# Four token tiles in flight in place of three in the first stage of a streaming encoder layer

## The chip, the core and the metric

The kernel runs on one core of a Trainium2 chip. The metric is the device time of one execution in microseconds (us). The five engines of the core are called TensorE (PE), VectorE (DVE), ScalarE (ACT), GpSimd (POOL) and SyncE (SP, which here issues all transfers). Each has its own queue and works through it in order.

## What is computed

One inference step of one layer over 1,024 prompt tokens and 32 sample tokens, 1,024 channels wide. Cut to what matters here:

```
h   = RMSNorm(x)                        # times the gains g_mix_norm
z   = h @ w_in                          # 1024 x 8192: q, k, v of both branches, gates
o_a = DiffAttn(h)                       # 8 heads, chunk-causal, two softmax maps per head
o_r = Retention(h)                      # 8 heads, rotary, chunkwise recurrent
x   = x + (sigmoid(g_a) * o_a + sigmoid(g_r) * o_r) @ w_o
x   = x + SwiGLU(RMSNorm(x))
x   = x + sigmoid(RMSNorm(x) @ w_ple_gate) * (p @ w_ple)
```

The outputs are the new x of all tokens, the new keys and values, and the retention states.

## The kernel before, in words

**Numbers.** Inputs are float32. For TensorE every operand is split into two float16 parts, a high one (a cast, mostly on ScalarE) and a low one (the rest, on VectorE), and a product takes three matmuls: high by high, high by low, low by high (lines 723, 724, 725). Each 256-column block of weights first needs a scale, from the sum of its squares (ScalarE, line 416, then a small matmul, line 300, and a chain of tiny VectorE instructions); then four parts of 512 columns per block are cast (ScalarE, line 462) and their low parts taken (VectorE, line 464).

**The stages.** The tokens stand in nine tiles of 128 rows (the last, of 32 rows, is the sample). For each of 8 heads, the program projects the tiles by the head's A half of w_in (q, k, v of the attention, q, k of the retention) and its B half (v of the retention and three gates), and does the attention and the retention of each tile. Then follow the products by w_o, the feed-forward part and the last gate. The change concerns the beginning: the stretch of some 85 us in which head 0 can work only on tiles that have been prepared.

**Preparing a token tile (`norm_x`, line 649).** The tile x*i* is loaded (line 662), squared and summed (ScalarE, 668), multiplied by the gains `gb` (GpSimd, 673; tile x0 alone on VectorE, 682), its inverse root taken (GpSimd, 758 and 759), scaled (ScalarE 687 or VectorE 689), transposed in two halves of four 128-column transposes each (TensorE, 697), and each half is cast (line 388) and its low part taken from PSUM (VectorE, 708). Slots for tiles lie in one weight buffer, `xw`: three for tiles and a fourth for `gb`. A tile waits for the tile three before it to be done, and, from x4 on, for the projection of tile *i*-4 (`("wait", ("pA", i - 3))`).

**What sets the order of the work.** The steps of all these parts are Python generators. A planner (`Flow`, line 86) runs them against its own clock: each step names an engine and an estimated cost, `("get", ...)` takes a buffer, `("wait", ...)` an event, `("delay", ...)` stands for a transfer's time, and of the steps that are ready the one that can start first is emitted, ties going to the lower priority number. So costs, delays and priorities decide only the order in which each engine's queue is written; the chip runs each queue in that order. Steps of a weight block take priority 2 as long as its due number lies more than 4 (`FAR`) ahead of the projection now under way, and -2 from then on (in `load_block_steps`). Projections of head 0 go A0, A1, A2, A3, A4, B0, A5, B1 and so on (`LAG` = 4): one of them is 8 steps of three matmuls.

Step counts below count these steps of three matmuls from the first projection on: A0 to A3 are steps 1 to 32, A4 is 33 to 40, and the 41st is B0's first. "Half" is one half of a token tile, four transposes.

## Time and profile before

| what | us |
|---|---|
| three timed runs, median (lowest to highest) | 1947.84 (1945.46 to 1948.18) |
| the profiled execution | 1947.6 |
| its span, first to last instruction | 1945.8 |
| TensorE busy in the span | 1885.6 (97%) |
| VectorE busy | 1531.5 (79%) |
| ScalarE busy | 1065.3 (55%) |
| GpSimd busy | 697.0 (36%) |

The span is what the trace covers; 1.8 us of the execution lie around it. The page of the profile divides the span into 40 slices of 48.6 us: TensorE is busy 5 tenths of the first, 8 of the second and 9 or more of all others but two in the middle, which belong to the passage into the feed-forward part. A view of stretches gives the same by any window, a view in order of time gives single instructions, and a view of waits says what ended an engine's idle time.

### The profile page before, as it was taken

To read this page: it belongs to the slowest core of one execution; us is meant where nothing else is said; L and a number is where in the kernel's file an instruction comes from. 1 tells how busy PE (TensorE), PEld (TensorE's weight loads), DVE (VectorE), ACT (ScalarE), POOL (GpSimd) and SP (SyncE) were. 2 spreads that over 40 slices of the span, in tenths; PEclk is the share of its full clock that TensorE was granted. 3 is DMA by queue.
4 is the path that set the end of the run, shared out by engine and by line. 5 is a ranking of instruction groups with operands and counts; after the bars stand their busy time and mean duration, and the time that the engine had idled before them with its cause. 6 is when DMAs were issued, how large, how long until landed. Compare 5 with 4: busy or idle time off the path is not lost.

```text
span 1945.8 us, 38415 instructions
## 1 busy us (share of the span) xinstructions
PE 1885.6 (97%) x14267; PEld 1216.2 (63%) x14267; DVE 1531.5 (79%) x3995; ACT 1065.3 (55%) x2775; POOL 697.0 (36%) x1142
## 2 busy tenths in 40 slices
PE   5899999999999999999999998899999999999999
PEld 2465565555655555556556685777777776666665
DVE  7887878788878788878888579999999986753364
ACT  6676767666666666666665346555555552111132
POOL 3754444344454444444543048323223210000010
PEclk9899999999999999999999999999999999999999
DMA  5221202112121121120213721122211107211031
GB/s 194 72 72 53 83 20 72 56 49 63 33 76 59 28 79 41 52 81 18 75 57 127 268 71 34 72 94 81 74 66 45 66 31 261 78 60 61 28 131 49
DMA packets 71949, 147.44 MB, mean 76 GB/s; under 512 B 25265, under 2 KB 52017, under 8 KB 63825
## 3 DMA queue, kind: packets, MB, share of 16 engines
q1 hardware_dynamic: 71760, 144.98, 22.3%
q8 instruction: 112, 1.84, 0.4%
q14 instruction: 77, 0.62, 0.1%
HBM read 113.61 MB, written 31.34 MB: 74 GB/s over the span
## 4 chain that ended last, share of the span: by engine, by line
PE 83%; DVE 10%; ACT 2%; POOL 2%; issue 2%; DMA 1%; SPq 0%; DVEq 0%; POOLq 0%; ACTq 0%
PE pj L723 10%; PE pj L725 9%; PE pj L724 9%; PE ps L471 9%; PE ps L473 9%; PE ps L472 9%; PE ps L1458 4%; PE ps L1456 4%; PE ps L1457 4%; PE t L907 2%; PE sc L860 2%; PE sc L863 1%; PE pj L734 1%; PE t L1055 1%; PE po L926 1%
## 5 line engine op out<-in xcount | busy, mean ns | idle before, releaser
L723 PE MATMUL pj<-w,xh 128*128 128x512 f16 x1024 | 390.6, 381 | 0.7 <-ACT w L462 0.7
L724 PE MATMUL pj<-w,xh 128*128 128x512 f16 x1024 | 389.8, 381 | 1.4 <-DVE w L464 1.4
L725 PE MATMUL pj<-w,xh 128*128 128x512 f16 x1024 | 389.8, 381 | 0.0
L471 PE MATMUL ps<-mixs,w 128*128 128x352 f16 (+1 forms) x960 | 260.6, 277 | 1.5 <-DVE pws L1336 1.5
L472 PE MATMUL ps<-mixs,w 128*128 128x352 f16 (+1 forms) x960 | 260.5, 276 | 0.3 <-POOL mixs L1482 0.3
L473 PE MATMUL ps<-mixs,w 128*128 128x352 f16 (+1 forms) x960 | 260.4, 276 | 0.0
L471 PEld LDWEIGHTS <-w 128*128 128x128 f16 x1728 | 169.7, 98 | 65.6 <-issue 7.0
L473 PEld LDWEIGHTS <-w 128*128 128x128 f16 x1728 | 169.4, 98 | 55.1 <-issue 4.2
L472 PEld LDWEIGHTS <-w 128*128 128x128 f16 x1728 | 169.5, 98 | 49.6 <-issue 0.8
L725 PEld LDWEIGHTS <-xh 128*128 128x128 f16 x1024 | 100.5, 98 | 124.3 <-DVE xh L708 2.5
L1591 POOL TENSOR_TENSOR st<-st 128x512 f32<-128x512 f32 x66 | 85.9, 1301 | 251.5 <-DVE w L1586 187.0
L723 PEld LDWEIGHTS <-xh 128*128 128x128 f16 x1024 | 101.3, 99 | 77.5 <-issue 1.1
L878 ACT ACTIVATE p<-sc,nb,scs 128x256 f32<-128x256 f32 (+7 forms) x128 | 106.1, 830 | 77.6 <-DVE nb L872 29.9
L472 PE MATMUL ps<-tT,w 128*128 128x352 f16 (+1 forms) x528 | 143.6, 277 | 3.6 <-DVE tT L1482 3.6
L724 PEld LDWEIGHTS <-xh 128*128 128x128 f16 x1024 | 100.5, 98 | 72.7 <-issue 0.8
L473 PE MATMUL ps<-tT,w 128*128 128x352 f16 (+1 forms) x528 | 143.7, 277 | 0.0
L471 PE MATMUL ps<-tT,w 128*128 128x352 f16 (+1 forms) x528 | 143.6, 277 | 0.0
L1586 DVE SCALAR_TENSOR_TENSOR w<-st,gus,w 128x512 f16<-128x512 f32 x132 | 140.4, 1064 | 0.1
L870 DVE TENSOR_REDUCE nm<-sc 128x1 f32<-128x768 f32 (+6 forms) x112 | 102.5, 916 | 27.0 <-PE sc L863 25.5
L1458 PE MATMUL ps<-a,w 128*128 128x352 f16 x312 | 97.5, 313 | 0.5 <-DVE w L1677 0.5
L1457 PE MATMUL ps<-a,w 128*128 128x352 f16 x312 | 97.5, 313 | 0.0
L1456 PE MATMUL ps<-a,w 128*128 128x352 f16 x312 | 97.5, 312 | 0.0
(433 smaller groups left out, 4890.0 us busy)
## 6 DMA issues: line engine op xcount, KB each, us to landing
st<-in_win_dram SPq DMA_DIRECT2D x30, 1024.0 KB, 4.9
st<-in_wgu_dram SPq DMA_DIRECT2D x22, 1024.0 KB, 4.9
st<-in_wdn_dram SPq DMA_DIRECT2D x16, 704.0 KB, 4.5
out_dram<-kv SPq DMA_DIRECT2D x64, 128.0 KB, 1.7
a_d<-a SPq DMA_DIRECT2D x9, 528.0 KB, 2.6
b<-a_d SPq DMA_DIRECT2D x9, 528.0 KB, 8.5
mixs<-mix_d SPq DMA_DIRECT2D x8, 528.0 KB, 6.2
pw_d<-pws SPq DMA_DIRECT2D x12, 352.0 KB, 5.6
```

What stands on the lines that cost most here:

```text
L471: nc.tensor.matmul(out=ps, lhsT=wh, rhs=ah, start=first, stop=False)
L472: nc.tensor.matmul(out=ps, lhsT=wh, rhs=al, start=False, stop=False)
L473: nc.tensor.matmul(out=ps, lhsT=wl, rhs=ah, start=False, stop=last)
L723: nc.tensor.matmul(out=ps, lhsT=xhi, rhs=w[:, k, 0], start=(k == 0), stop=False)
L724: nc.tensor.matmul(out=ps, lhsT=xhi, rhs=w[:, k, 1], start=False, stop=False)
L725: nc.tensor.matmul(out=ps, lhsT=xh[:, k, 1, t0:t0 + P], rhs=w[:, k, 0], start=False, stop=(k == KD - 1))
L870: nc.vector.tensor_reduce(out=nm[0:R, mc], in_=pv, axis=AX.X, op=ALU.max, negate=True)
L878: nc.scalar.activation(pt[0:R, 0:NK], ps[0:R, p0:p0 + NK], AF.Exp, bias=nb[0:R, m:m + 1], scale=sc_ap[0:R], accum_out=Z[0:R, m:m + 1])
L1456: nc.tensor.matmul(out=ps, lhsT=wt[:, 0, j], rhs=a[:, 0, cs], start=(first and j == js[0]), stop=False)
L1457: nc.tensor.matmul(out=ps, lhsT=wt[:, 1, j], rhs=a[:, 0, cs], start=False, stop=False)
L1458: nc.tensor.matmul(out=ps, lhsT=wt[:, 2, j], rhs=a[:, 1, cs], start=False, stop=(last and j == js[-1]))
L1586: nc.vector.scalar_tensor_tensor(out=w[:, i, 1], in0=src, scalar=s, in1=w[:, i, 0], op0=ALU.mult, op1=ALU.subtract)
```

## The change

In `norm_x`, four slots hold token tiles, so a tile waits for the one four before it, and the wait for the projection is gone; the gains lie in the buffer that later holds the cached keys of the sample (`kcs`), so the first writing of that buffer now waits for the last token tile. The load of the first B weights waits until tile x3 has landed, and their due number is 9 where it was 4, so that their steps keep priority 2 during steps 1 to 40. The planner takes 3.0 in place of 2.0 for the time of a weight block's or a token tile's transfer. The loads of some small constants (`const_b`) are no longer held until x0 has been scaled, but until it is done.

```
--- before.py
+++ after.py
@@ -402,7 +402,7 @@
         else:
             yield DM(1.0)
             nc.sync.dma_start(out=st, in_=src)
-            yield ("delay", 2.0)
+            yield ("delay", 3.0)
         norm = rowf is None and not tail
         am4 = sm(4, "wam4", 3)
         am8 = sm(8, "wam8%d" % b, 1) if rowf is not None else None
@@ -526,7 +526,7 @@
         nc.gpsimd.memset(s02[64:128], 0.0)
 
         xw = wtile().bitcast(F32)
-        gb = xw[:, 3 * D:4 * D]
+        gb = hp.tile([P, 4, PAST], F16, tag="kcs", name="gb").rearrange("p m c -> p (m c)").bitcast(F32)
         xdone = []
         gsc = ca.tile([P, 3], F32, name="gsc")
 
@@ -568,7 +568,7 @@
 
         def const_b():
 
-            yield ("wait", ("n", 0))
+            yield ("wait", ("x", 0))
             yield ("get", "th")
             yield ("get", "z")
             rows_sb = wk.tile([P, 3, P], F32, tag="th", name="th").rearrange("p a c -> p (a c)")
@@ -649,18 +649,17 @@
         def norm_x(i):
 
             R = P if i < NT - 1 else TS
-            if i > 2:
-                yield ("wait", ("x", i - 3))
             if i > 3:
-                yield ("wait", ("pA", i - 3))
+                yield ("wait", ("x", i - 4))
             if i == 2:
                 yield DM(0.3)
                 nc.sync.dma_start(out=cs_sb, in_=rot)
             yield ("get", "xc")
-            xf = xw[:, i % 3 * D:(i % 3 + 1) * D]
+            xf = xw[:, i % 4 * D:(i % 4 + 1) * D]
             yield DM(R / 256.0)
             nc.sync.dma_start(out=xf[0:R], in_=xN[i, 0:R])
-            yield ("delay", 2.0)
+            yield ("delay", 3.0)
+            yield ("set", ("xd", i))
             yield ("get", "p")
             yield S(D, 0.1)
             sq = pp_.tile([P, 1024], F32, tag="p", name="xsq")
@@ -826,8 +825,7 @@
             nc.vector.tensor_scalar(out=do_s, in0=p2[:, 1:2], scalar1=lun, scalar2=_f(2.0 ** -14), op0=ALU.mult, op1=ALU.mult)
             vsc = sm(1, "vsc")
             nc.vector.tensor_tensor(out=vsc, in0=dA[1], in1=s[:, 1:2], op=ALU.mult)
-            if h:
-                yield ("wait", ("av", h - 1, NT - 1))
+            yield ("wait", ("av", h - 1, NT - 1) if h else ("x", NT - 1))
             kcs = hp.tile([P, 4, PAST], F16, tag="kcs", name="kcs")
             vcs = hp.tile([P, 4, 2, P], F16, tag="vcs", name="vcs")
             for m in range(2):
@@ -1232,6 +1230,8 @@
         def load_w(h, ab, res, prio, split=False):
 
             def steps(b0, b1):
+                if ab and not h:
+                    yield ("wait", ("xd", 3))
                 if b0 == 0:
                     yield ("get", "w")
                     res.extend(pair_tile())
@@ -1239,7 +1239,7 @@
                 yield ("wait", ("wt", ab, h))
                 for b in range(b0, b1):
                     yield from load_block_steps(win[h, 2 * ab + b], res[0], b, 0, "wAB"[1 + ab], None, res[1],
-                                                due=h * NT + ab * LAG)
+                                                due=h * NT + ab * (LAG if h else 9))
                     yield ("set", ("w", ab, h, b))
             if split:
                 flow.add(steps(0, 1), prio)
@@ -1417,7 +1417,7 @@
                 flow.add(ple(part), 6)
 
         flow = Flow(dict(pj=3, sc=1, o=3, p=5, A=5, B=3, w=3, st=2, mix=4, z=3, kv=3, rot=2, sqz=2, qst=2, q4=2, aT=2, of=2,
-                         ret=2, th=2, xc=3, su=1))
+                         ret=2, th=2, xc=4, su=1))
         flow.buffers["w"].pop()
         with tc.manual_schedule(engines={mybir.EngineType.PE, mybir.EngineType.DVE, mybir.EngineType.Activation,
                                          mybir.EngineType.Pool}):
```

The engines' queues change as follows at the three places that the prediction speaks of. TensorE's queue, where it passes from the fourth projection to the fifth (rows of line 697, 696 after the change, are transposes of token tiles, the others projections); first before, from the end of step 31 on:

```order
L725 LDWEIGHTS xh
L725 MATMUL pj<-w,xh 128x512
L723 LDWEIGHTS xh
L723 MATMUL pj<-w,xh 128x512
L724 LDWEIGHTS xh
L724 MATMUL pj<-w,xh 128x512
L725 LDWEIGHTS xh
L725 MATMUL pj<-w,xh 128x512
L697 MATMUL t<-cst_sb,w 128x128 x16
L723 LDWEIGHTS xh
L723 MATMUL pj<-w,xh 128x512
L724 LDWEIGHTS xh
```

and with the change, from the end of step 34 on:

```order
L724 LDWEIGHTS xh
L724 MATMUL pj<-w,xh 128x512
L696 MATMUL t<-cst_sb,w 128x128 x4
L722 LDWEIGHTS xh
L722 MATMUL pj<-w,xh 128x512
L723 LDWEIGHTS xh
L723 MATMUL pj<-w,xh 128x512
L724 LDWEIGHTS xh
L724 MATMUL pj<-w,xh 128x512
L696 MATMUL t<-cst_sb,w 128x128 x8
L722 LDWEIGHTS xh
L722 MATMUL pj<-w,xh 128x512
```

Before, a block of sixteen transposes (four halves, x4's first) stands in one piece behind step 32. With the change, halves of x4 and x5 stand singly behind steps 21, 29, 31 and 34, and a block of eight (two halves) behind step 35.

GpSimd's queue behind its first pair of roots (lines 673 and 672 are the multiplications of a token tile by the gains, 758, 759 and 757, 758 the roots of tiles, 959 to 967 the rotary of head 0); before:

```order
L673 TENSOR_TENSOR w<-w 128x1024
L758 TENSOR_SCALAR xss<-xss 128x1
L759 TENSOR_TENSOR xnr<-xss,neghalf 128x1
L673 TENSOR_TENSOR w<-w 128x1024
L758 TENSOR_SCALAR xss<-xss 128x1
L759 TENSOR_TENSOR xnr<-xss,neghalf 128x1
L673 TENSOR_TENSOR w<-w 128x1024
L758 TENSOR_SCALAR xss<-xss 128x1
L759 TENSOR_TENSOR xnr<-xss,neghalf 128x1
L959 TENSOR_TENSOR ta<-zr,cs_sb 128x128
L963 TENSOR_TENSOR tb<-zr,cs_sb 128x128
L965 TENSOR_TENSOR qk<-ta,tb 128x2x32
```

and with the change:

```order
L672 TENSOR_TENSOR w<-w,gb 128x1024 x2
L757 TENSOR_SCALAR xss<-xss 128x1
L758 TENSOR_TENSOR xnr<-xss,neghalf 128x1
L672 TENSOR_TENSOR w<-w,gb 128x1024
L757 TENSOR_SCALAR xss<-xss 128x1
L758 TENSOR_TENSOR xnr<-xss,neghalf 128x1
L757 TENSOR_SCALAR xss<-xss 128x1
L758 TENSOR_TENSOR xnr<-xss,neghalf 128x1
L672 TENSOR_TENSOR w<-w,gb 128x1024
L757 TENSOR_SCALAR xss<-xss 128x1
L758 TENSOR_TENSOR xnr<-xss,neghalf 128x1
L672 TENSOR_TENSOR w<-w,gb 128x1024
```

The multiplications of x1 and x2 now stand together, those of x3, x4 and x5 follow, all ahead of any rotary; before, a tile's rotary stood behind the fourth root.

VectorE's queue in the middle of the A weights' low parts (line 464, `A0s` and `A1s` for the two blocks; 708 and 707 are low parts of token halves, 689 and 688 a tile's scaling); before:

```order
L708 TENSOR_TENSOR xh<-t,xh 128x4x128
L583 TENSOR_SCALAR gS<-gS 128x8
L464 SCALAR_TENSOR_TENSOR w<-st,A0s,w 128x2x256
L464 SCALAR_TENSOR_TENSOR w<-st,A1s,w 128x2x256
L585 TENSOR_SCALAR gd<-gd 128x1
L678 TENSOR_SCALAR xrg<-xnr,gsc 128x1
L589 TENSOR_REDUCE gam<-th 128x2
L464 SCALAR_TENSOR_TENSOR w<-st,A0s,w 128x2x256
L464 SCALAR_TENSOR_TENSOR w<-st,A1s,w 128x2x256
L708 TENSOR_TENSOR xh<-t,xh 128x4x128
L464 SCALAR_TENSOR_TENSOR w<-st,A0s,w 128x2x256
L464 SCALAR_TENSOR_TENSOR w<-st,A1s,w 128x2x256
```

and with the change:

```order
L464 SCALAR_TENSOR_TENSOR w<-st,A1s,w 128x2x256
L388 CAST xh<-t 128x4x128
L464 SCALAR_TENSOR_TENSOR w<-st,A0s,w 128x2x256
L464 SCALAR_TENSOR_TENSOR w<-st,A1s,w 128x2x256
L707 TENSOR_TENSOR xh<-t,xh 128x4x128
L560 CAST id_88<-cst_sb 128x128
L464 SCALAR_TENSOR_TENSOR w<-st,A0s,w 128x2x256
L464 SCALAR_TENSOR_TENSOR w<-st,A1s,w 128x2x256
L677 TENSOR_SCALAR xrg<-xnr,gsc 128x1
L688 TENSOR_SCALAR w<-w,xrg 128x1024
L464 SCALAR_TENSOR_TENSOR w<-st,A1s,w 128x2x256
```

The scaling of x1 has come into VectorE's queue ahead of the last low part, and a first instruction on a constant (line 583) has gone behind them.

## Rows read from the trace of the kernel before

**Rows 1.** First line of the page.
```profile
span 1945.8 us, 38415 instructions
```

**Rows 2.** Stretches: from:to, length, busy us of each engine, clock of TensorE, transfers.
```profile
core 0: us, PE busy (x) PEld busy (x) DVE busy (x) ACT busy (x) POOL busy (x), PEclk, DMA share, GB/s
20.00:80.00 60.00, 47.20 (x237) 24.54 (x237) 54.21 (x136) 41.30 (x100) 39.04 (x48) 0.94 0.35 119
50.00:60.00 10.00, 4.23 (x23) 2.74 (x22) 8.17 (x24) 4.56 (x10) 9.43 (x10) 0.85 0.74 258
60.00:70.00 10.00, 9.36 (x48) 4.97 (x46) 8.32 (x14) 4.51 (x11) 8.70 (x14) 0.81 0.13 40
70.00:80.00 10.00, 7.64 (x53) 4.58 (x54) 9.16 (x29) 8.49 (x30) 6.81 (x12) 1.00 0.05 16
80.00:90.00 10.00, 9.93 (x69) 6.41 (x69) 9.04 (x32) 6.87 (x23) 8.09 (x18) 0.83 0.07 26
85.00:120.00 35.00, 34.93 (x233) 20.00 (x232) 32.95 (x101) 27.89 (x75) 17.75 (x34) 1.00 0.22 67
130.00:1080.00 950.00, 942.17 (x6923) 549.76 (x6922) 768.80 (x2336) 617.05 (x1828) 432.16 (x853) 1.00 0.19 60
```

**Rows 3.** TensorE in order of time: start, length, what, idle before and its releaser.
```profile
40.17 0.60 PE L697 MATMUL t<-cst_sb,w 128*128 128x128 f32 x4
...
53.01 1.09 PE L697 MATMUL t<-cst_sb,w 128*128 128x128 f32 x8 [1.85 <-ACT w L687]
...
57.65 1.09 PE L697 MATMUL t<-cst_sb,w 128*128 128x128 f32 x4 [3.55 <-DVE w L689]
...
59.11 1.09 PE L697 MATMUL t<-cst_sb,w 128*128 128x128 f32 x4 [0.37 <-DVE w L689]
...
62.55 1.06 PE L697 MATMUL t<-cst_sb,w 128*128 128x128 f32 x4
...
63.83 0.38 PE L724 MATMUL pj<-w,xh 128*128 128x512 f16 x1
64.04 0.38 PE L725 MATMUL pj<-w,xh 128*128 128x512 f16 x1
```

**Rows 4.** GpSimd in order of time: multiplications of token tiles by the gains.
```profile
16.40 2.35 POOL L673 TENSOR_TENSOR w<-w 128x1024 f32<-128x1024 f32 x1 [8.49 <-ACT xsq L668]
...
50.86 4.66 POOL L673 TENSOR_TENSOR w<-w 128x1024 f32<-128x1024 f32 x2
```

**Rows 5.** VectorE in order of time: instructions beside those of GpSimd, and free ones.
```profile
17.88 1.42 DVE L464 SCALAR_TENSOR_TENSOR w<-st,A0s,w 128x512 f16<-128x512 f32 x1
...
20.48 2.25 DVE L583 TENSOR_SCALAR gS<-gS 128x8 f32<-128x8 f32 x1
...
27.07 0.74 DVE L464 SCALAR_TENSOR_TENSOR w<-st,A1s,w 128x512 f16<-128x512 f32 x1
...
29.82 0.69 DVE L708 TENSOR_TENSOR xh<-t,xh 128x512 f16<-128x512 f32 x1 [0.48 <-ACT xh L388]
...
31.01 2.41 DVE L617 TENSOR_TENSOR z<-z 128x128 f32<-128x128 f32 x1
...
46.37 2.56 DVE L464 SCALAR_TENSOR_TENSOR w<-st,B0s,w 128x512 f16<-128x512 f32 x1 [0.28 <-ACT w L462]
...
53.93 1.68 DVE L1113 TENSOR_SCALAR grn<-grn,hdB 128x128 f32<-128x128 f32 x1
...
66.08 2.58 DVE L1028 TENSOR_TENSOR z<-z,gqk 128x256 f32<-128x256 f32 x1
```

**Rows 6.** ScalarE in order of time: a weight part, a tile's scaling, a tile's square.
```profile
20.17 0.71 ACT L462 ACTIVATE w<-st,A0s 128x512 f16<-128x512 f32 x1
...
24.27 1.15 ACT L687 ACTIVATE w<-w,xrg 128x1024 f32<-128x1024 f32 x1 [1.07 <-DVE xrg L678]
...
44.54 1.10 ACT L668 ACTIVATE xsq<-w 128x1024 f32<-128x1024 f32 x1
```

**Rows 7.** What TensorE waited for, 0 to 140 us: total, times, longest.
```profile
PE t L697 <- DVE xh L708: 1.6, 1, 1.6
```

More of the change, by code (lines that the diff above doesn't have):

```diff
@@ L404, in load_block_steps @@
             nc.sync.dma_start(out=st, in_=src)
-            yield ("delay", 2.0)
+            yield ("delay", 3.0)
         norm = rowf is None and not tail
@@ L528 @@
         xw = wtile().bitcast(F32)
-        gb = xw[:, 3 * D:4 * D]
+        gb = hp.tile([P, 4, PAST], F16, tag="kcs", name="gb").rearrange("p m c -> p (m c)").bitcast(F32)
         xdone = []
@@ L569, in const_b @@
         def const_b():
-            yield ("wait", ("n", 0))
+            yield ("wait", ("x", 0))
             yield ("get", "th")
@@ L651, in norm_x @@
             R = P if i < NT - 1 else TS
-            if i > 2:
-                yield ("wait", ("x", i - 3))
             if i > 3:
-                yield ("wait", ("pA", i - 3))
+                yield ("wait", ("x", i - 4))
             if i == 2:
@@ L659, in norm_x @@
             yield ("get", "xc")
-            xf = xw[:, i % 3 * D:(i % 3 + 1) * D]
+            xf = xw[:, i % 4 * D:(i % 4 + 1) * D]
             yield DM(R / 256.0)
             nc.sync.dma_start(out=xf[0:R], in_=xN[i, 0:R])
-            yield ("delay", 2.0)
+            yield ("delay", 3.0)
+            yield ("set", ("xd", i))
             yield ("get", "p")
@@ L828, in cache_steps @@
             nc.vector.tensor_tensor(out=vsc, in0=dA[1], in1=s[:, 1:2], op=ALU.mult)
-            if h:
-                yield ("wait", ("av", h - 1, NT - 1))
+            yield ("wait", ("av", h - 1, NT - 1) if h else ("x", NT - 1))
             kcs = hp.tile([P, 4, PAST], F16, tag="kcs", name="kcs")
@@ L1234, in steps @@
             def steps(b0, b1):
+                if ab and not h:
+                    yield ("wait", ("xd", 3))
                 if b0 == 0:
@@ L1241, in steps @@
                     yield from load_block_steps(win[h, 2 * ab + b], res[0], b, 0, "wAB"[1 + ab], None, res[1],
-                                                due=h * NT + ab * LAG)
+                                                due=h * NT + ab * (LAG if h else 9))
                     yield ("set", ("w", ab, h, b))
@@ L1419 @@
         flow = Flow(dict(pj=3, sc=1, o=3, p=5, A=5, B=3, w=3, st=2, mix=4, z=3, kv=3, rot=2, sqz=2, qst=2, q4=2, aT=2, of=2,
-                         ret=2, th=2, xc=3, su=1))
+                         ret=2, th=2, xc=4, su=1))
         flow.buffers["w"].pop()
```

## Prediction

> **What bounds the kernel now.** I read the stretches first. From 130 to 1080 us TensorE is busy 942 of 950 us [rows 2]: head by head, TensorE is the bound, and nothing moved there can change much. The first 130 us are different. From 20 to 80 us it is busy only 47.2 of 60 us, while VectorE is busy 54.2 [rows 2]. By tens, TensorE idles 5.8 us in 50 to 60, 0.6 in the next ten, 2.4 in 70 to 80, and its mean clock is 0.85, 0.81 and, in 80 to 90, 0.83 [rows 2]. The clock has two levels here, 1.2 and 2.4 GHz, so 0.85 means that 3.0 of the 10 us passed at the lower one, and 0.81 that 3.8 did.
>
> Next, TensorE in order of time shows what the hole is. It has done steps 1 to 32 when it comes to the block of token transposes; it idles 1.85, 3.55 and 0.37 us there, each time for the scaling of a tile [rows 3]. Behind the wait of 3.55 us the clock is at its lower level: a half takes 1.09 us, where one at 40.17 took 0.60, and still 1.06 at 62.55; at 63.83 a matmul is back at 0.38 [rows 3]. Behind the wait of 1.85 us eight transposes still took 1.09 together, which is the full clock [rows 3]. So the hole costs 5.8 us of idling, plus half of the 5.8 us or so that TensorE worked at the low clock between 57.7 and 63.8: **8.7 us** in all. The tiles are late because x4's square ran at 44.54 [rows 6], behind all of B's squares, and GpSimd's multiplications of x5 and x6 only from 50.86 [rows 4]. The second hole (0.6 and 2.4 us of idling in 60 to 80 [rows 2], 1.6 of it for the low part of a token half [rows 7], then 3.4 us at the low clock, 1.7 us lost) costs **4.7 us**. From 85 to 120 TensorE idles 0.1 of 35 us, but VectorE is at 32.95 [rows 2]: there VectorE only just keeps up.
>
> Last, VectorE beside GpSimd. A low part of weights (line 464) takes 0.74 us at 27.07, but 1.42 at 17.88 and 2.56 at 46.37; a constant of 8 columns takes 2.25, one of 128 columns 2.41 and 1.68, a product of 256 columns 2.58 [rows 5]. Each of these ends with, or one own length after, a GpSimd multiplication of 2.35 us [rows 4, 5]. Instructions that read PSUM, as line 708, take their usual 0.69 throughout. In sum 10.6 us of VectorE's time before 69 us is such blocking. The Trainium skill, "SBUF — State Buffer", section "Who interferes with whom", has it as a rule: VectorE and GpSimd share a port pair that one instruction holds to its end, and an instruction with two SBUF inputs or in a two-port mode waits. The rows agree; the rule speaks against a change that packs GpSimd's multiplications into the time of weight conversion, and is priced as a rival below.
>
> **The change, part by part.** The work is the same, and from the feed-forward part on all queues are the same. So I place the changed queues on a time line by hand, with durations from the rows. All times of the changed program are such estimates.
>
> *A weights later: loss 2.0.* ScalarE's squares now come between the weight parts (1.10 against 0.71 us each [rows 6]), and the first runs behind a weight part. GpSimd multiplies x1 from about 17.8 us and x2 right behind, x3 from about 24.9. VectorE has behind it mainly line 464; three of them get blocked, for about 0.8, 2.3 and 2.3 us, where before one did and the useless constant of line 583 took the other blow. One low part got in between two GpSimd instructions at the end of the row at 46.37, so I let them alternate. VectorE's own work from 17.1 us to the last low part is eight low parts at 0.74 and four halves' casts and low parts at 0.69 [rows 5], less the 0.07 by which neighbours overlap, 0.67 for x1's scaling and some 0.6 of tiny ones: 9.1 us. With 5.4 blocked it ends near 31.5; before it ended at 27.8 [rows 5]. So x1 is scaled and transposed at 30.7 to 31.8. From there 12 steps (0.65 each at full clock, three starts some 0.215 apart [rows 3]) and 5 halves (0.43 from start to start, the rest of the 0.60 being tail) are left to step 16, 10.0 us, and 0.8 for the clock: 42.6. Before, step 16 and as many halves were done at 40.6 [rows 3].
>
> *The hole of 50 to 64 goes: gain 8.7.* x4's square now stands ahead of B's squares, at about 34.8; GpSimd is free and done with it at 38.4. x5's scaling is through at 52.5. TensorE needs x4 at 45.9 (step 21) and x5 at 54.4 (step 31).
>
> *New waits: loss 6.4.* x4's scaling on VectorE meets x5's multiplication and ends at 46.3: 0.4. GpSimd multiplies x6 and x7 one behind the other from about 51.0 to 55.7 and takes their roots until 57.3 and later; two of B's low parts are blocked for 1.1 and 1.7 us meanwhile, and x6 is scaled at 59.4 to 60.5. TensorE is there at 57.4 (behind step 35): 3.1. This is nearer to the wait that lowered the clock (3.55) than to the one that did not (1.85), so I add the same low clock, 2.9. Bounds: none of the three, if VectorE runs 3 us ahead of my line, and 10 us if x7 is waited for as well.
>
> At step 40 that makes 8.7 - 6.4 - 2.0 = 0.3, and the changed queue has one half more behind it (0.4): **0.7 us** ahead.
>
> *The second hole: gain 2.8.* VectorE stands better than TensorE. By its 136th row, at 68.7 us before and some 68.5 now, it has done about 4.0 us more (four token casts, copies, operands of the scores) and left 1.3 us undone: 2.7 ahead, against TensorE's 0.7. The waits of 3.0 us there shrink by the difference, 2.0, and I take half of the low clock with them, 0.8. Bounds: nothing, or all 4.7.
>
> *At nothing:* B's first weights wait for x3's landing, but in SyncE's queue of either program x3's load stands ahead of theirs, which also wait for the stage buffers; x3's load now stands ahead of three constants' loads, which are first used behind the A weights; the cached keys' buffer is written behind step 78 of TensorE's queue, the last tile is transposed by step 48; the delays of 3.0 us only order. TensorE's queue has as many rows as before. In heads 2 to 8 the queues are shuffled (some small VectorE work goes to ScalarE and GpSimd, at most 65% busy there [rows 2]); TensorE idles 7.8 of 950 us there [rows 2], so this is worth -2 to +2, taken as 0.
>
> **Sum:** 0.7 + 2.8 = 3.5 us off the profiled execution of 1947.6 (span 1945.8 [rows 1] and 1.8 around it): **1944.1 us**. That execution lies 0.2 below the median of the three runs, 1947.84. From 85 us on the gain passes to the end only as far as VectorE is ahead as well, and it is 2.7 to 3.5 us ahead; so the sum is near what this stage can carry.
>
> **The rivals.**
> *The hole closes with no new wait.* For it: x6 misses its place by 3 us only, and a line worked by hand is no better than that. Against it: VectorE's load in 85 to 120. 8.7 + 0.4 - 2.0, and 1 to 3 at the second hole, make 8 to 10, of which VectorE may hold back some: about 1939.5.
>
> *The hole only moves.* The wait for x6 also lasts for x7, and the second hole stays: 0.7 + 0, with a us either way: 1947. That the delay of B's weights does nothing, as said, belongs here: then only the order of the squares is left of the change.
>
> *GpSimd locks VectorE out, and it ends slower.* The place is B's low parts and the scalings beside GpSimd's eight multiplications, 8 x 2.35 = 18.8 us. If each blocks in full, that is 8.2 us more than the 10.6 now; VectorE's idling of 5.8 us in 20 to 80 [rows 2] can take up some 3 of them. The rest, 5.2, is TensorE's: about 1953. It decides from about 14 us of blocked time on; my line has 11.4 (0.8, 2.35, 2.3, 0.9, 1.1, 1.7 and 2.2 for x8's). The skill's rule above, taken with back-to-back multiplications that let nothing in between, would do just this. Against it: VectorE got in between at 48.4, and a good part of its work reads PSUM.
>
> **How the numbers follow.** A measurement of this kernel tells 0.2% (3.9 us) from no change. Forecast 0.5, with 3 us of error either way, so that half of it lies beyond the bound; hole closed 0.2; hole moved 0.2; locked out 0.1, nearly all of it slower by over 0.2%. Faster: 0.25 + 0.19 = 0.44; same: 0.25 + 0.01 + 0.2 = 0.46; slower 0.10. The range takes in the closed hole and the moved one and leaves half of each outer tail: 1938.5 to 1950.0.
>
> **What would show it.** In the changed profile: VectorE's last low part of A at 31 us or later, with lengths over 2 us beside GpSimd; x4's square near 35 us; no idling of TensorE at 51 to 57 us, but a wait of some 3 us for a scaled tile behind step 35 near 58 us with the low clock behind it; waits under 1.5 us between 68 and 80. The forecast is wrong if the A weights are ready by 28 us, if TensorE runs from 43 to 70 us without a wait over 1 us, or if from 85 to 130 us TensorE now idles by more than a few tenths, since then VectorE took the gain back.

## The result, and the profile after

| | before | after |
|---|---|---|
| timed runs, median (lowest to highest), us | 1947.82 (1945.27 to 1948.95), 6 runs | 1955.01 (1953.40 to 1957.58), 6 runs |
| span of the profiled execution | 1945.8 | 1953.6 |
| ratio to before, 95% interval | | 1.0041 (1.0028 to 1.0054) |

The changed kernel is slower by 7.2 us, 0.41%; 1944.1 had been forecast, and the range ended at 1950. Line numbers of the changed kernel lie up to 2 below those shown of before (line 697 is now 696, 708 is 707, 1218 is 1216); line 464 keeps its number.

The stretches of the changed kernel, to be held against [rows 2]:

```profile
core 0: us, PE busy (x) PEld busy (x) DVE busy (x) ACT busy (x) POOL busy (x), PEclk, DMA share, GB/s
20.00:80.00 60.00, 46.89 (x237) 24.67 (x237) 55.67 (x143) 41.79 (x100) 41.68 (x52) 0.97 0.33 116
50.00:60.00 10.00, 8.50 (x46) 4.45 (x44) 9.24 (x13) 5.59 (x9) 9.43 (x11) 1.00 0.00 0
60.00:70.00 10.00, 6.76 (x36) 4.23 (x37) 9.96 (x21) 7.88 (x22) 8.06 (x13) 0.83 0.70 250
70.00:80.00 10.00, 8.06 (x58) 4.65 (x57) 9.81 (x40) 7.38 (x25) 6.52 (x15) 1.00 0.09 29
...
85.00:120.00 35.00, 33.79 (x208) 18.05 (x206) 30.46 (x97) 27.84 (x77) 16.84 (x33) 1.00 0.23 67
130.00:1080.00 950.00, 940.07 (x6918) 549.54 (x6918) 751.40 (x2283) 619.13 (x1836) 440.87 (x890) 1.00 0.19 59
```

The hole of 50 to 60 us is gone (8.50 busy against 4.23), but 60 to 70 now has one, with the low clock. From 85 to 120 TensorE idles 1.2 us where it idled 0.1, with VectorE less busy than before. From 130 to 1080 it idles 9.9 us in place of 7.8. (The clock column counts the time ahead of a trace's first clock record, which starts at 34.9 us here and at 29.7 before, as full. The matmuls of 512 columns up to there take some 0.6 us in both traces, and 0.38 behind it: they ran at the low clock.)

TensorE in order of time in the first stage (start, duration, what it does, and the idle time ahead of it with its releaser); beside [rows 3]:

```profile
start us, us, engine line op out<-in xcount [idle before <-releaser]
23.82 0.58 PE L723 MATMUL pj<-w,xh 128*128 128x512 f16 x1 [3.93 <-DVE w L464]
27.83 0.58 PE L723 MATMUL pj<-w,xh 128*128 128x512 f16 x1 [1.29 <-DVE w L464]
30.80 1.12 PE L696 MATMUL t<-cst_sb,w 128*128 128x128 f32 x4 [0.68 <-DVE w L688]
...
47.50 0.63 PE L696 MATMUL t<-cst_sb,w 128*128 128x128 f32 x4 [0.40 <-DVE w L688]
...
62.46 1.97 PE L696 MATMUL t<-cst_sb,w 128*128 128x128 f32 x8 [3.95 <-ACT w L686]
...
80.27 0.83 PE L1053 MATMUL t<-id,qst 128*128 128x128 f16 x12 [1.99 <-ACT of L937]
```

The first weights and x1 come late, x4 costs 0.40, x6 costs 3.95 and the low clock behind it (eight transposes took 1.97, where eight took 1.09 at 53.01 before [rows 3]), and a wait of 1.99 stands at 80 us. GpSimd's multiplications by the gains, to be held against [rows 4]:

```profile
18.11 5.11 POOL L672 TENSOR_TENSOR w<-w,gb 128x1024 f32<-128x1024 f32 x2 [10.02 <-ACT xsq L667]
24.48 2.75 POOL L672 TENSOR_TENSOR w<-w,gb 128x1024 f32<-128x1024 f32 x1
...
52.24 4.85 POOL L672 TENSOR_TENSOR w<-w,gb 128x1024 f32<-128x1024 f32 x2
...
57.80 0.93 POOL L758 TENSOR_TENSOR xnr<-xss,neghalf 128x1 f32<-128x1 f32 x1
```

Three multiplications now stand beside the A weights; the last row is x6's root. VectorE's instructions of that time and from 46 to 61 us, beside [rows 5]:

```profile
19.45 1.56 DVE L464 SCALAR_TENSOR_TENSOR w<-st,A0s,w 128x512 f16<-128x512 f32 x1
20.93 2.84 DVE L464 SCALAR_TENSOR_TENSOR w<-st,A1s,w 128x512 f16<-128x512 f32 x1
24.30 0.73 DVE L464 SCALAR_TENSOR_TENSOR w<-st,A0s,w 128x512 f16<-128x512 f32 x1
24.95 2.83 DVE L464 SCALAR_TENSOR_TENSOR w<-st,A1s,w 128x512 f16<-128x512 f32 x1
...
30.66 0.74 DVE L464 SCALAR_TENSOR_TENSOR w<-st,A1s,w 128x512 f16<-128x512 f32 x1
...
45.79 1.57 DVE L688 TENSOR_SCALAR w<-w,xrg 128x1024 f32<-128x1024 f32 x1
...
52.55 2.33 DVE L1024 TENSOR_TENSOR z<-z,qkr 128x256 f32<-128x256 f32 x1
...
55.40 2.24 DVE L464 SCALAR_TENSOR_TENSOR w<-st,B0s,w 128x512 f16<-128x512 f32 x1
...
61.02 0.20 DVE L677 TENSOR_SCALAR xrg<-xnr,gsc 128x1 f32<-128x1 f32 x1
```

Two low parts of A take 2.84 and 2.83 where 0.74 is their own length, and the last one ends at 31.4.

**Where the 7.8 us of span went.** The queues are in another order, so the same instruction at two times says little. I use TensorE's *lost time* at a landmark: its time less the plain work that stands ahead of it in the queue, each kind of matmul taken at its median distance from start to start between 200 and 1050 us. Landmarks are the starts of the sample tile's projections, one for each half of each head (16 in all: near 129 us the A half of head 0, near 321 the second of head 1, near 1056 the last). It is an estimate from the traces, and two kernels with the same queues behind 129 us give it within 0.5 us from there to 1056. Ahead of 129 us it is good to some 2.5 us only: `e2`, `p1`, `p_b_m29` and `e2_d4` below have the queue of before up to 66 us or longer and gave 43.3, 42.7, 43.4 and 41.1 at that landmark, before 43.6.

| stretch | lost before | lost after | difference |
|---|---|---|---|
| up to 85 us | 41.3 | 40.2 | -1.1 |
| 85 to the landmark at 129 | 2.3 | 4.2 | +1.9 |
| 129 to 321 (rest of head 0, head 1) | 10.2 | 13.4 | +3.2 |
| 321 to 1056 | 45.3 | 46.0 | +0.7 |
| from there to the end of the span | 1846.7 | 1849.8 | +3.1 |

(The last row is the span less the lost time so far.) Up to 85 us the changed kernel is 1.1 us ahead, which is within that spread and not the 3.5 that were forecast; the loss lies behind it, where the prediction had put nothing.

### The profile page after: what moved, and what is told of

It is laid out like the page before. It is cut to its first block, busy times and chain, and to the rows that moved or that the text cites. A ratio compares the mean times of both kernels' runs of the same rounds, so it can differ in the third digit from the quotient of the medians.

```text
span 1953.6 us, 38420 instructions
## 1 busy us (share of the span) xinstructions
PE 1888.6 (97%) x14267; PEld 1217.8 (62%) x14267; DVE 1516.2 (78%) x3947; ACT 1070.6 (55%) x2788; POOL 703.6 (36%) x1177
## 4 chain that ended last, share of the span: by engine, by line
PE 75%; DVE 11%; POOL 5%; ACT 5%; issue 2%; DMA 1%; SPq 0%; POOLq 0%; DVEq 0%; ACTq 0%
PE ps L471 9%; PE ps L473 9%; PE ps L472 9%; PE pj L722 8%; PE pj L723 7%; PE pj L724 7%; PE ps L1458 4%; PE ps L1456 4%; PE ps L1457 4%; PE sc L858 1%; ACT p L876 1%; PE t L905 1%; PE sc L861 1%; DVE w L464 1%; PE t L1053 1%
```

## The experiments

All tables give medians of timed runs and ratios to runs of the kernel before on the same chip in the same session, and lost times from one profile each. "Heads 2 and 3" in some expectations means the stretch from 129 to 321 us.

### Delay or first stage? Four kernels

My theories were H (the planner's delay of 3.0 in the weight blocks of all heads shuffled heads 1 to 8), S (the first stage's end state carries on) and N (any new plan, that is, any new order of the queues, lands anywhere).

`e1_heads_delay2`, the changed kernel with this edit:

```
-            yield ("delay", 3.0)
+            yield ("delay", 3.0 if tag == "B" and due == 9 else 2.0)
```

> The changed kernel with the assumed landing delay of weight blocks back at 2.0 in heads 1 to 8 and behind them; head 0 and so the first 90 us of all queues stay the changed ones. Theory H (the delay of 3.0 shuffled the small work of heads 2 to 8 and of the passage, and that cost 3.9 us from 129 to 1056 us and 3.0 behind): about 7 us come back, 1947 to 1949 us, the sample tile of head 0 still near 129.2. Theory S (the first stage leaves VectorE behind, and head 2 pays for it): it stays at 1953 to 1956 us, with TensorE again waiting some 2 us in 190 to 270. Theory N (any new plan of the heads lands anywhere within some 4 us): neither end, the waits at places that neither kernel had.

`e2_heads_delay3`, the kernel before with the reverse:

```
-            yield ("delay", 2.0)
+            yield ("delay", 2.0 if tag == "B" and due == LAG else 3.0)
```

> The kernel before with the delay 3.0 for weight blocks of heads 1 to 8 and behind alone; its first 100 us are untouched. Theory H: 1951 to 1955 us, with no difference up to 130 us. Theory S: 1947 to 1949 us. Theory N: anywhere from 1944 to 1955.

`p1_margin31`, the kernel before with a meaningless edit (`MARGIN` is what the planner adds before a step that moves to TensorE):

```
-MARGIN = 0.3
+MARGIN = 0.31
```

> The kernel before with the planner's margin for a matmul at 0.31 in place of 0.30: no meaning of its own, it only gives another plan from about 75 us to the feed-forward part. Theory N: off 1947.8 by 2 to 4 us either way, with TensorE idling in heads 2 to 8 by some us more or less than the 7.8 of before. Theories H and S: within 1 us of 1947.8, since the delay or the first stage is what matters.

`e3_blocks_delay2`, the changed kernel with 2.0 for all weight blocks:

```
-            yield ("delay", 3.0)
+            yield ("delay", 2.0)
```

> The changed kernel with the delay of weight blocks at 2.0 everywhere, head 0's B half too. Theory H: as the first experiment, 1947 to 1949, and since B's casts now come earlier in the queues, the first stage moves by 1 us or less at the sample tile of head 0. Theory S: 1953 to 1956 us. Theory N: off the first experiment by some us though the heads' delay is the same.

| kernel | median us | ratio (95%) | lost at 129 | 129 to 321 | 321 to 1056 |
|---|---|---|---|---|---|
| before | 1948.72 | | 43.6 | 10.2 | 45.3 |
| e1 | 1949.77 | 1.0003 (0.9994 to 1.0012) | 42.7 | 11.3 | 46.1 |
| e2 | 1952.73 | 1.0022 (1.0013 to 1.0031) | 43.3 | 12.5 | 46.0 |
| p1 | 1949.28 | 1.0002 (0.9993 to 1.0011) | 42.7 | 12.3 | 45.5 |
| e3 | 1951.27 | 1.0013 (1.0005 to 1.0022) | 42.8 | 11.6 | 45.9 |

Taking the delay out gave back 5 us and putting it in cost 4: a mirror image, and theory H looked shown, though e1 and e3 came out 0.8 and 2.3 us above its range. The one thing against it was the neutral kernel, which lost 12.3 us between 129 and 321 without any delay of 3.0 (though its total hardly moved). I came back to that below.

### GpSimd's multiplications taken out, or moved to VectorE

`f1_after_nomult` and `f2_before_nomult` drop one line each, so that tiles x1 to x8 stay without their gains, and keep the plan:

```
-                nc.gpsimd.tensor_tensor(out=xf[0:R], in0=xf[0:R], in1=gb[0:R], op=ALU.mult)
```

> The changed kernel with the eight GpSimd multiplications of token tiles 1 to 8 by the gains left out (those tiles stay without their gains), the plan and all queues otherwise the same. Theory L (GpSimd's instructions lock VectorE out, and this makes the A weights late and x6 wait): line 464 never over 1 us, the last low part of A before 28 us, the wait for x6 near 62 us gone, TensorE at 85 us some 5 to 8 us ahead of the changed kernel. Theory W (the waits come from the order of the queues): the wait for x6 stays above 2 us. And for what reaches the end: theory P (a gain of the first stage passes through) 1946 to 1949 us; theory G (VectorE gives it back between 85 and 260 us) 1951 to 1954 us.

> The kernel before with the same eight multiplications left out, its plan otherwise untouched. Theory L: the waits for x5 and x6 in 50 to 60 us shrink, since these tiles no longer wait for GpSimd, and TensorE at 85 us is 4 to 8 us ahead of before. Theory W: the hole stays, as x4's square stands behind B's squares, and less than 3 us come. At the end: theory P 1940 to 1944 us; theory G 1946 to 1948.

`v_b_stt` (from before) and `v_e1_stt` (from e1) multiply and scale all tiles on VectorE; in `norm_x`:

```
-            if i:
-                yield ("wait", ("n", 0))
-                yield G(D)
-                nc.gpsimd.tensor_tensor(out=xf[0:R], in0=xf[0:R], in1=gb[0:R], op=ALU.mult)
...
-            if i == 0:
+            if True:
                 yield ("wait", "gb")
                 yield V(D, 1.0, 0.06)
                 nc.vector.scalar_tensor_tensor(out=xf[0:R], in0=xf[0:R], scalar=rg[0:R], in1=gb[0:R], op0=ALU.mult, op1=ALU.mult)
-                yield ("set", ("n", 0))
+                if i == 0:
+                    yield ("set", ("n", 0))
```

> The kernel before with the gains of token tiles 1 to 8 multiplied in on VectorE, together with the scaling, in one instruction each as for tile 0, and nothing on GpSimd for them. VectorE takes on some 8 x 0.6 us or more of work of its own, and loses the 10 us of blocking. Theory L: VectorE is no worse off, the first 85 us are shorter by 2 to 6 us; theory W: they are the same or longer by what VectorE takes on, up to 5 us. At the end, by theory P the same difference, by theory G within 2 us of before. The queues of all heads are planned anew, so 1 or 2 us either way are noise of that.

> The changed kernel with the delay of 2.0 for the weight blocks of heads 1 to 8, as in the first experiment, and the gains multiplied in on VectorE as above. Theory L and P: 2 to 6 us under the first experiment's 1949.8, so it beats before. Theory G: within 2 us of 1949.8. Theory W: over 1951.

| kernel | median us | ratio (95%) | lost at 129 | 129 to 321 | 321 to 1056 |
|---|---|---|---|---|---|
| before | 1947.86 | | 43.6 | 10.2 | 45.3 |
| f1 (after, no multiplications) | 1940.68 | 0.9961 (0.9946 to 0.9976) | 32.2 | 13.3 | 45.6 |
| f2 (before, no multiplications) | 1942.10 | 0.9969 (0.9956 to 0.9982) | 36.3 | 10.2 | 45.4 |
| v_b | 1949.01 | 1.0006 (0.9996 to 1.0016) | 40.9 | 10.8 | 45.4 |
| v_e1 | 1947.78 | 0.9998 (0.9989 to 1.0008) | 39.2 | 13.0 | 45.9 |

Three things follow.

*The multiplications cost TensorE 12.2 us in the changed kernel (44.4 to 32.2) and 7.3 before (43.6 to 36.3).* Beside them, line 464 takes up to 2.84 us; in f1 up to 75 us it never exceeds 0.92. Held one by one against f1 and f2, whose VectorE queues are the same, VectorE's instructions up to the sample tile's last low part are 10.8 us longer in the changed kernel and 10.4 before. So nearly the same blocking goes with 4.9 us more of TensorE's time, since it now falls on what TensorE waits for. The Trainium skill, "SBUF — State Buffer", section "Who interferes with whom", names the lock between these two engines; these rows agree. TensorE's waits between 16 and 130 us (line, what released it, us in total, times, longest) in the changed kernel:

```profile
engine line waited for: us in total, times, longest us
PE pj L723 <- DVE w L464: 5.2, 2, 3.9
PE t L696 <- ACT w L686: 4.0, 1, 4.0
PE t L1053 <- ACT of L937: 2.0, 1, 2.0
...
PE pj L722 <- ACT w L462: 1.6, 1, 1.6
```

and in f1:

```profile
PE t L1052 <- ACT of L936: 2.0, 1, 2.0
PE pj L721 <- ACT w L462: 1.6, 1, 1.6
PE pj L722 <- DVE w L464: 1.0, 1, 1.0
PE t L695 <- ACT w L685: 0.7, 1, 0.7
```

The waits for line 464 and for x6 shrink from 9.2 to 1.7; the wait of 1.6 for line 462 and that of 2.0 for `of` stay, so these are the order's own and not the lock's. f1 and f2 take away two things at once, the lock and GpSimd's own time on a tile's path. At the A weights it is the lock: line 464 reads nothing that GpSimd writes, and its own instructions are the long ones. Of the 3.95 us for x6 some 2.3 are the lock's, by an estimate: x6's root was done at 58.73, but VectorE came to it only at 61.02, behind two instructions that had been lengthened by 1.9 and 1.5 us. The rest is GpSimd's own time. Between f1 and f2 the change's order is worth some 4 us at the landmark: the idea was sound, and the multiplications ate it.

*A gain of the first stage passes through to the end.* f1 is 12.2 ahead of the changed kernel at 129 us and still 12.7 at 1056; f2 is 7.3 and 7.2 ahead of before. Theory G falls. (f1 came out 5 us under theory P's own range, as 12 us had come by 85 us in place of 5 to 8.) Moved to VectorE and not dropped, the multiplications leave 2.7 us less lost time at 129 in v_b than before and 3.5 less in v_e1 than in e1. The median of v_e1 is 2.0 us under e1's; that of v_b is 1.2 above before, as its profile is its fastest run, 2.3 us under the median.

*The loss behind 129 us goes with the queue, not with the first stage.* In 190 to 270 us, the changed kernel and f1, whose first stage is 12 us shorter:

```profile
190.00:270.00 80.00, 77.88 (x615) 46.29 (x614) 61.69 (x177) 52.41 (x155) 37.68 (x74) 1.00 0.18 57
```

```profile
190.00:270.00 80.00, 77.87 (x554) 44.76 (x552) 61.66 (x169) 51.23 (x146) 37.65 (x76) 1.00 0.14 42
```

and before:

```profile
190.00:270.00 80.00, 79.98 (x634) 47.79 (x633) 63.36 (x185) 55.58 (x161) 34.68 (x75) 1.00 0.17 56
```

TensorE idles 2.12 and 2.13 us there (before 0.02), with the same waits to the tenth. Theory S falls. What they wait for is seen in TensorE's waits from 130 to 1056 us, in the changed kernel:

```profile
PE t L1216 <- DVE mx L1211: 3.5, 10, 0.7
...
PE t L1216 <- POOL mx L1211: 1.1, 2, 0.9
```

and before:

```profile
...
PE t L1218 <- POOL mx L1213: 1.4, 5, 0.3
PE pj L750 <- DVE su L747: 0.8, 2, 0.4
PE t L1218 <- DVE mx L1213: 0.3, 1, 0.3
```

In this plan TensorE waits 4.6 us for the mixed output `mx`, mostly from VectorE, in place of 1.7, mostly from GpSimd.

### One part of the change alone, and two tiles at a time

`c1_four_only` has the four tiles and, of the other parts, only the later wait of `const_b` (in the core):

```
-            if i > 2:
-                yield ("wait", ("x", i - 3))
             if i > 3:
-                yield ("wait", ("pA", i - 3))
+                yield ("wait", ("x", i - 4))
...
-            xf = xw[:, i % 3 * D:(i % 3 + 1) * D]
+            xf = xw[:, i % 4 * D:(i % 4 + 1) * D]
```

> The kernel before with the four token tiles in flight alone (the fourth buffer, the gains in another buffer, tile i waiting for tile i - 4); all delays 2.0 and B's first weights as before. I count TensorE's lost time at the sample tile of head 0: the start of its matmuls less the plain work that stands ahead of it in the queue (43.6 us before, 44.4 after, 32.2 after and 36.3 before without GpSimd's multiplications). Theory L (more of GpSimd's multiplications early, beside the A weights, lock VectorE out): the first token halves are late by 2 us or more, as in the changed kernel, and the lost time at the sample tile is 42 to 45. Rival O (the fourth tile is the gain, and B's later weights the cost): under 41. From 129 to 321 us the queues are of the family of the margin experiment, which lost 12.3 us there against 10.2 before: so 1947 to 1951 us in all by theory L.

`c2_B_only` holds back B's weights and does no more:

```
+                if ab and not h:
+                    yield ("wait", ("xd", 3))
...
-                                                due=h * NT + ab * LAG)
+                                                due=h * NT + ab * (LAG if h else 9))
```

> The kernel before with B's first weights held back alone (they wait for x3's landing and are due at 9); three tiles in flight, delays 2.0. Theory L: the A half's early steps are as before, since the first multiplications stand where they stood; the hole at 50 to 64 us shrinks as x4's square no longer stands behind B's squares, but x5 and x6 are still multiplied late: lost time at the sample tile 41 to 44. Rival O: over 44, as B's half starts later with nothing gained. In all 1946 to 1951 us, 2 of it a new plan of heads 2 and 3.

`m_e1_56` and `m_e1_12` are e1 with two tiles' gains on VectorE, as `v_e1_stt` has for all:

```
-            if i:
+            if i and not (i in (5, 6)):
...
-            if i == 0:
+            if i == 0 or i in (5, 6):
```

and with `i < 3` in place of `i in (5, 6)`.

> The first experiment's kernel (1949.8 us, lost time 42.7 at the sample tile) with the gains of tiles 5 and 6 alone multiplied in on VectorE. TensorE's queues agree with it but for the place of some token halves. Theory L: GpSimd's pair of 4.85 us ahead of the wait for x6 is gone, so that wait of 3.96 us falls under 1.5 and with it the low clock behind it (1 us): lost time 38 to 40.5, and 1945 to 1947.5 us in all, under before. Theory W (the waits come from the order of the queues): the wait moves by less than 1 us, and the lost time stays at 42 to 43.5.

> The first experiment's kernel with the gains of tiles 1 and 2 alone multiplied in on VectorE, so that GpSimd is idle beside most of the A weights. Theory L: the last low part of A before 29 us in place of 31, the token half 2 at 28 us or earlier in place of 30.4, the wait for x6 as before or smaller; lost time at the sample tile 39.5 to 41.5. Theory W: the A weights are as late as in the first experiment, for the squares are what holds them; lost time 42 or more. In all 1946 to 1949 us by L, since the plan of heads 2 and 3 is new here (spread of that so far 10.2 to 13.4 us lost from 129 to 321).

| kernel | median us | ratio (95%) | lost at 129 | 129 to 321 | 321 to 1056 |
|---|---|---|---|---|---|
| before | 1947.74 | | 43.6 | 10.2 | 45.3 |
| c1 | 1950.49 | 1.0012 (1.0002 to 1.0021) | 43.9 | 11.5 | 45.5 |
| c2 | 1952.70 | 1.0022 (1.0013 to 1.0031) | 42.3 | 12.7 | 46.5 |
| m_e1_56 | 1947.68 | 1.0002 (0.9993 to 1.0012) | 41.6 | 11.5 | 45.7 |
| m_e1_12 | 1948.93 | 1.0004 (0.9994 to 1.0013) | 37.9 | 12.0 | 46.5 |

The four tiles alone bring nothing that shows (43.9): the multiplications come early and lock the A weights (4.6 us of waits for line 464), while x4 is still late (6.5). The first rows of c1's waits between 16 and 130 us:

```profile
PE t L695 <- DVE w L687: 6.5, 1, 6.5
PE pj L722 <- DVE w L464: 4.6, 2, 3.5
```

With B's weights alone 42.3 us are lost, 1.3 less than before, which is within the spread. Both lost times fell within what theory L gave. The totals went up with the plans, that of c2 1.7 us above its range. With x5 and x6 on VectorE the wait for x6 is gone, as expected, but smaller ones take its place (1.9, 2.1 and 1.5 us), so 1.1 us come and not 2 to 4: a miss, and no more than the spread. With x1 and x2 there, no low part of A in the stretch takes over 0.75, the first A weights are ready without a wait for line 464, and x1 is transposed at 24.01 in place of 30.35. The lost time of 37.9 is better than expected, but this profile flatters it: from 27.8 us on it was at the full clock up to 130, which no other profile here was, and the other runs of the kernel say less (last section).

### What is the plan worth? Six kernels

`p_a_m31` is the changed kernel with `MARGIN = 0.31`, `p_b_m29` the kernel before with 0.29, `m_e1_12_m31` the kernel `m_e1_12` with 0.31; `e2_d4` is e2 with 4.0 where it had 3.0:

```
-            yield ("delay", 2.0)
+            yield ("delay", 2.0 if tag == "B" and due == LAG else 4.0)
```

> The changed kernel with the planner's margin at 0.31, a perturbation without meaning; the delay of 3.0 stays everywhere. Lost time of TensorE between the sample tiles at 129 and 321 us: 13.4 in the changed kernel, 10.2 before, 10.8 to 13.0 in eight other plans. Theory H (the delay of 3.0 itself costs): still 12.5 to 14, and the total within 2 us of 1955. Theory N (a new plan is a new draw): anywhere in 10 to 14, the total 1950 to 1957.

> The kernel before with the margin at 0.29, again without meaning, all delays 2.0. Theory H: as before, lost time between 129 and 321 us of 10 to 11, 1947 to 1949 in all. Theory N: 10 to 14, most likely 12, and 1948 to 1952, since before lies at the lower end of all plans so far.

> The kernel before with the delay of weight blocks of heads 1 to 8 at 4.0 in place of 2.0 (the second experiment had 3.0, 1952.7 us, and lost 12.5 us between 129 and 321). Theory H: more than at 3.0, 13.5 or over, and 1953 to 1957 in all. Theory N: another draw, 10 to 13.5, 1948 to 1953.

> The kernel with the gains of tiles 1 and 2 on VectorE (lost time 37.9 at the sample tile, 1948.9 us median) with the margin at 0.31: its queues of heads 2 and 3 then agree from some 190 us on with the plan that lost 10.8 to 11.6 us between 129 and 321, in place of 12.0. Theory N: a draw near 11, 1 us less than without, 1946 to 1949 us. Theory H: no difference, 1948 to 1950.

The last two put a first stage without GpSimd's multiplications ahead of the two best plans: `q_eall_m29` is `v_e1_stt` with `MARGIN = 0.29`, `q_ball_d4` is `v_b_stt` with the delay of `e2_d4`.

> Four tiles in flight with all gains on VectorE (lost time 39.2 at the sample tile), delay 2.0 in the heads, margin 0.29: from 196 us on its TensorE queue is that of the p_b_m29 kernel, which lost 52.2 us from 129 to 1056 (before 55.5, changed kernel 59.4). If the two parts add (a gain of the first stage passes through, and a plan's cost goes with the plan): 4 us under p_b_m29's 1943.7, 1939 to 1941.5 us, and under both kernels. If plans cost what they cost only beside their own first stage: 1943 to 1948.

> Three tiles in flight with all gains on VectorE, delay 4.0 in the heads: from 196 us or a little later its TensorE queue is that of e2_d4 (lost 51.4 us from 129 to 1056; lost time at the sample tile 41.1, and 40.9 in the like of this one with delay 2.0). If the parts add: 1942 to 1944 us, as e2_d4. If not: 1945 to 1950.

| kernel | median us | ratio (95%) | lost at 129 | 129 to 321 | 321 to 1056 |
|---|---|---|---|---|---|
| before (first four kernels, last two) | 1948.55, 1949.24 | | 43.6 | 10.2 | 45.3 |
| p_a_m31 | 1950.54 | 1.0009 (1.0000 to 1.0018) | 43.9 | 12.9 | 45.7 |
| p_b_m29 | 1943.67 | 0.9972 (0.9963 to 0.9982) | 43.4 | 9.9 | 42.2 |
| e2_d4 | 1943.26 | 0.9972 (0.9959 to 0.9984) | 41.1 | 11.2 | 40.2 |
| m_e1_12_m31 | 1944.26 | 0.9979 (0.9970 to 0.9988) | 39.7 | 9.9 | 45.8 |
| q_eall_m29 | 1941.28 | 0.9962 (0.9948 to 0.9975) | 40.4 | 11.1 | 42.4 |
| q_ball_d4 | 1941.96 | 0.9968 (0.9956 to 0.9980) | 41.2 | 11.8 | 40.4 |

Theory H falls: a delay of 4.0 makes the kernel *faster* by 5 us, and a hundredth in the margin takes 5 us off the kernel before and 4 off the changed one (1950.54 against 1955.01, in another session). p_a_m31 alone would have left H standing for its stretch: it lost 12.9 us from 129 to 321, as H had it, and its gain lies behind 1056. Theory N holds in that the plan counts and no one delay does: from 129 to 1056 us the kernels lost between 51.4 and 59.4 us, the kernel before 55.5, the changed kernel 59.4, the most of all. Its ranges were too narrow: p_b_m29, e2_d4 and m_e1_12_m31 came out 2 to 5 us under the lowest that either theory gave.

The plans are far fewer than the kernels. Held row by row, TensorE's queues between 330 and 455 us are six: e2 and f1 have that of the changed kernel, f2 that of before, q_eall_m29 that of p_b_m29, q_ball_d4 that of e2_d4, p_a_m31 its own, and the other ten kernels, all with a delay of 2.0 in the later heads, share one, which before's joins at 455. From 321 to 1056 us the three queues of before, of the changed kernel and of the ten lost 45.3 to 46.5, p_a_m31 45.7, p_b_m29's 42.2 and 42.4, e2_d4's 40.2 and 40.4. Most of what else sets the kernels apart lies in 129 to 321 us, where the queues still differ: 9.9 to 13.4, and pairs with the same queue there (before and f2, the changed kernel and f1, e1 and m_e1_56) agree within 0.2.

The parts nearly add up: the plan of p_b_m29 lost 52.2 beside its own first stage and 53.5 beside that of q_eall_m29, the plan of e2_d4 51.4 and 52.1 beside that of q_ball_d4. Both totals lie in or at the range expected of a sum. q_eall_m29 is the fastest kernel that computes everything, 0.38% below before and 13.7 us under the changed kernel's median. The stretches of q_eall_m29 (first) and of p_b_m29:

```profile
20.00:80.00 60.00, 49.13 (x261) 26.09 (x262) 56.20 (x164) 48.13 (x117) 28.68 (x53) 0.97 0.34 119
...
321.00:1056.00 735.00, 729.95 (x5362) 428.17 (x5361) 595.75 (x1796) 476.82 (x1416) 335.65 (x679) 1.00 0.18 57
```

```profile
20.00:80.00 60.00, 46.41 (x238) 24.19 (x237) 54.63 (x138) 41.36 (x100) 39.55 (x48) 0.94 0.35 121
...
321.00:1056.00 735.00, 730.06 (x5400) 428.40 (x5397) 596.20 (x1796) 476.12 (x1416) 336.04 (x682) 1.00 0.18 57
```

In the first stage TensorE is busy for 2.7 us more and GpSimd for 11 us less; the later heads are alike.

## Why the prediction was wrong, step by step

The forecast took 3.5 us off the span, and it grew by 7.8. Of the 11.3 us between them 2.4 lie in the first 85 us, 5.8 from there to 1056, and 3.1 behind.

*A weights later, loss 2.0: right in its cause, about 1 us too small.* The line had VectorE's three blocked low parts at 0.8, 2.3 and 2.3; they were 0.8, 2.1 and 2.1 (1.56, 2.84, 2.83 less 0.74). The last low part ended at 31.4, forecast 31.5; x1 was transposed from 30.80, forecast 30.7. But by step 16 the changed kernel was 3.1 us behind by lost time: TensorE stayed at the low clock until 34.9 us (before, until 29.7), and the line had allowed 0.8 for that. In e1 and p_a_m31, with the same queue so far, it was 2.1 and 2.4. c1 and m_e1_12 bear out the cause, since the A weights are late where the early multiplications stand on GpSimd and on time where they do not.

*The hole of 50 to 64 goes, gain 8.7: right.* x4's square ran at 34.54 (forecast 34.8), and TensorE has no wait from 47.50 to 58.5.

*New waits, loss 6.4: right in sum.* From step 16 to step 40 the changed kernel lost 6.2. x4 cost 0.40 (forecast 0.4), x6 3.95 (forecast 3.1), and the low clock behind it lasted from 62.2 to 65.6, 1.7 us lost (forecast 2.9). At about step 40 the changed kernel was 0.3 behind (lost time 35.9 against 35.5), where 0.7 ahead had been forecast.

*Second hole, gain 2.8: half of it.* From there to 85 us it gained 1.4 (lost time 35.9 to 40.2, before 35.5 to 41.3). The wait of 1.99 at 80.27 for `of`, which ScalarE writes, was not on my line; as f1 keeps it, it belongs to the order.

*"From 85 us on the gain passes to the end only as far as VectorE is ahead as well": the wrong limit.* Gains of 7.3 and 12.2 us passed whole in f2 and f1. The 1.9 us lost from 85 to 129 are the plan's: f1 loses there 4.2, as the changed kernel, f2 2.2, as before.

*"In heads 2 to 8 the queues are shuffled", "worth -2 to +2, taken as 0": the step that failed.* It cost 3.9 us from 129 to 1056, 5.8 with the stretch from 85 on. I took TensorE's idling of 7.8 us in 950 [rows 2] as all that a plan could win or lose. But idling is not the whole price of a plan: of the 4.1 us by which the plan of e2_d4 beats before's, TensorE's idling from 130 to 1056 shows 2.2 (4.14 us against 6.36), and the rest lies in time that counts as busy (first before, then e2_d4):

```profile
130.00:1056.00 926.00, 919.64 (x6739) 534.73 (x6739) 751.23 (x2281) 603.89 (x1793) 428.68 (x846) 1.00 0.17 54
```

```profile
130.00:1056.00 926.00, 921.85 (x6780) 540.86 (x6779) 746.89 (x2283) 611.36 (x1810) 427.33 (x848) 1.00 0.18 57
```

Against the 55.5 of before the kernels lost from 4.1 less to 3.9 more. So the term should have been 4 to either side; where its middle lies, six queues don't tell. The changed kernel drew the upper end, 3.2 of its 3.9 in 129 to 321.

*"From the feed-forward part on all queues are the same", so nothing: wrong by 3.1 us, 1.7 of them open.* 1.7 of it came by 1090 us, in the passage, where the queues still differ, and 1.3 between 1180 and 1240. The 1.3 go with the clock and not with the plan: there the changed kernel's profile has three stretches at the low clock and before's two, but f2, with the queues of before, has three as well and loses 1.1. The 1.7 stay open: e2 lost 1.2 there, while f1, whose queues are those of the changed kernel, gained 0.4, and p_a_m31 gained 1.3, so neither the order nor the delay alone makes it.

*The rivals.* The lock rival had the right sign and nearly the right time (1953), but that was luck: VectorE was blocked for 10.8 us, near my line's 11.4 and well under the 14 from which it was to decide. It was the place and not the sum that counted. That a loss could come from behind the first stage was no rival at all.

*The signs.* A low part ending at 31 or later, lengths over 2 us, x4's square near 35, no idling at 51 to 57, the wait for x6 with the low clock: all came. So did one against it, the 1.2 us of idling in 85 to 120, though VectorE was less busy there than before and f1 loses as much.

## What to carry to other kernels

Where a planner writes the queues, a change of a cost, a delay or a buffer can draw a new plan far behind the place that it was made for; give that its own term, as wide as a few meaningless perturbations show it to be (here 8 us, twice the gain that was in question). Look how many different queues they really give, and never read an edit and its undoing as proof without such a neutral kernel beside them. Price a lock between two engines by what waits for the blocked instruction, not by the sum of blocked time. And when a stage is improved, try the neutral perturbations too: p_b_m29 and e2_d4 brought as much as the change was meant to.

## What was not expected of the hardware

*The clock differs from run to run of one kernel.* The first 285 matmuls of TensorE's queue, up to 84 us, are the same in the changed kernel and in e1, and so are the waits between them at the start. In the changed kernel's profile the matmuls behind the wait of 1.29 us take 0.63 us, the low clock, and they do so up to 34.7 us:

```profile
27.83 0.58 PE L723 MATMUL pj<-w,xh 128*128 128x512 f16 x1 [1.29 <-DVE w L464]
28.21 0.63 PE L724 MATMUL pj<-w,xh 128*128 128x512 f16 x1
...
35.02 0.38 PE L724 MATMUL pj<-w,xh 128*128 128x512 f16 x1
```

In e1's the same matmuls take 0.38, the full clock; it is low again behind the next wait, and full from 33.4 on:

```profile
27.37 0.38 PE L723 MATMUL pj<-w,xh 128*128 128x512 f16 x1 [1.29 <-DVE w L464]
27.59 0.38 PE L724 MATMUL pj<-w,xh 128*128 128x512 f16 x1
...
31.68 0.63 PE L723 MATMUL pj<-w,xh 128*128 128x512 f16 x1
...
33.39 0.38 PE L724 MATMUL pj<-w,xh 128*128 128x512 f16 x1
```

It goes with the time of a whole run. The ten runs of m_e1_12 split by the mean clock: three at 0.996 or 0.997 took 1945.1 to 1947.0 us, seven at 0.994 or 0.995 took 1948.8 to 1950.4. Its profile is one of the three. So a kernel with such waits has more than one time, and a lost time from one profile of it is good to some 3 us only (the profiles of v_b, e2_d4 and c2 lie 2.0 to 2.3 us under the median of their runs); f1, whose waits there are short, kept its four runs within 1 us.
